# A state-space layer whose elementwise steps take one operand from PSUM, in a new order of steps

## The chip, the cores and the metric

The kernel runs on one core of a Trainium2 chip. The engines that matter are TensorE (PE, with its weight loads PEld), VectorE (DVE), ScalarE (ACT), GpSimd (POOL) and SyncE (SP), which issues DMAs. Each engine runs its own instructions in their order; between engines, semaphores make one wait for another. The metric is the time of one execution on the device, in microseconds: the median of three runs.

## The reference

The kernel computes a trunk of two layers on 512 tokens of 1024 features: a mixer, a layer norm, a SwiGLU feed-forward part and a layer norm, twice. The mixer of the second layer is attention; that of the first is the state-space layer to which the change is confined. Cut to what matters:

```python
mag = exp(lam_re * dt); lbar = mag * (cos, sin)(lam_im * dt)       # 64 groups, 64 complex states each
coef = (lbar - 1) / lam;  bb = coef * b
bu = einsum('blgh,gph->lbgp', u, bb)                                # 16 inputs a group
s  = associative_scan(s_t = lbar * s_{t-1} + bu_t)                  # along the 512 positions
y  = Re(einsum('lbgp,ghp->blgh', s, c)) + d_skip * x
h  = gelu(y); val, gate = split(h @ w_glu, 2); z = val * sigmoid(gate)
mix = z @ w_out
```

## The kernel before

Positions are cut into 64 chunks of 8. Within a chunk the output comes from a kernel K_t = Re(C lambda^t B) of 8 lags; from chunk to chunk the state is carried by a scan. Groups are handled in 4 blocks of 8 groups a half (`GB` = 8). The tiles have 128 partitions and 1024 floats, and one such step on DVE handles one tile.

For each block b, the function `ssm` (L460) has small functions that each issue one step. `f_g` (L617) and `f_h` (L626) make the tables G = powers x B and H = powers x C, two parts each (letters g, j and h, i); each part is an outer product, three DVE instructions (`outer`, L597): a product into the tile, a second product into a scratch tile `u`, their sum. `p_t` transposes G on PE (letters t, T; L636, the copy back on ACT L637). `p_m` (m, M; L647) multiplies it with the input into PSUM banks 2 and 3. `p_k` (k; L673) computes the kernel, ACT copies it to the tile `ksb` (L680), POOL adds the diagonal, and SP writes it to DRAM (`kd`, L682). `f_n` (n; L690, L696) reads it back with 8 DMAs of shifted rows (16 for block 3). `f_e` (e; POOL, L466 by a helper) makes the exponentials, `f_r` (r) rotates PSUM's v by them on DVE, and `f_s` (s) runs the scan (L742), a POOL memset of the first column (L745), and four products and sums into the state tile `s`. `p_y` (y; L766) multiplies states and kernels into y, in PSUM banks 4 and 5, ACT copies it to `ysb` (L774). `p_z` (z; L781) transposes back, ACT applies gelu (L786) and rounds to the high part `xh` (L789); `f_l` (l) makes the low part `xl` on DVE. B stands for the powers of the later blocks (DVE), b for the exponentials' tables of the later blocks (`levels`, POOL, L1144).

Between these steps the dense product of the GLU starts. It comes in 32 quarters (an output tile and two feature tiles), and a product of float32 numbers is three matmuls: high x high, low x high, high x low (L292 to L294). The weights are read as chunks of 512 KB, two quarters each; ACT makes the high part (`wh`, L228) and DVE the remainder (`wl`, L231): letter p. The letter u1 runs one item of `GLU_FIRST` in banks 6 and 7 with copies to SBUF (L818); w0 and w2 run one that stays in PSUM. The rest of the quarters, the sigmoid and the split of the result follow in `ssm_end` (L879), where remainders are on POOL; then `proj` (the output product, L311 to L313) and all that follows.

The order of all this is written by hand: `SSM_ORDER` is a string of steps, a letter and a block each, and for PE, DVE, ACT, POOL and SP the instructions are issued in exactly the order in which the string calls the functions (`tc.manual_schedule`). An SBUF slot comes from a ring of 37 and is waited for when the ring hands it out again.

Of the kernel before, what the change touches and what calls it, by code (L numbers as in the profile page):

```python
# [244 lines left out]
class Trunk:  # L245
    def __init__(self, tc, io, ctx):
# [213 lines left out]
    def ssm(self):  # L460
        """The state-space layer, its GLU and output product. State rows are (half of the groups, p);
        blocks of GB groups of either half give the feature tiles b and 4 + b."""
# [146 lines left out]
        def tab(t, b):
            return (t[0], slice(0, GB)) if b == 0 else (t[GB], slice((b - 1) * GB, b * GB))  # L610

        def f_g(b, c=0, ns=None):
            gs = slice(b * GB, b * GB + GB)
# [1 line left out]
            if len(g) <= c:
                g.append(ring.get("g", F32))
            n0 = st[b].get(("n", c), 0)  # L617
            ns = slice(n0, ns or L)
            outer(g[c], (gt_[:, 0, gs], gt_[:, 1, gs]), (bre, bim), gs, c, 1, ns)
            st[b]["n", c] = ns.stop  # L620
# [8 lines left out]
        def p_t(b, c=0):
            """Transposes of G's part c."""  # L630
            g = st[b]["g"]
            gt = st[b]["gt", c] = ring.get("gt", F32)
            for hf in range(2):
                pt = self.ps[:, hf].rearrange("p (j m) -> p j m", j=4)
                for j in range(4):
                    nc.tensor.transpose(out=pt[:, j], in_=g[c][:, (hf * 4 + j) * 128:(hf * 4 + j + 1) * 128], identity=ident)  # L636
# [598 lines left out]
```

## Time and profile before

| | |
|---|---|
| time of one execution, median of 3 | 1273.83 us (1273.69 to 1274.01) |
| profiled execution, its span | 1271.4 us |
| outside the span (median less span) | 2.4 us |
| busy: PE, DVE, ACT, POOL | 1189.0, 691.3, 421.5, 224.2 us |
| state-space stage, up to the last product of y | 178.2 us |

PE is busy for 94% of the span. The stage of the state-space layer is the first seventh of it. A row of the timeline reads: start in us, length, engine, line, operation, output <- inputs, in brackets the idle time ahead of it and what ended it. In the prediction the lines of before are numbers of the old file; the changed file's numbers are 2 to 6 larger for the same code.

### The profile page before, as it was taken

The page shows a single profiled execution, that of the slowest core. Times are in us where ns is not written, and L with a number is a line of the kernel's source. Part 1 is how long each engine was busy: PE and PEld are TensorE (multiplying, and loading weights), DVE is VectorE, ACT ScalarE, POOL GpSimd, SP SyncE. Part 2 cuts the span into 40 slices and gives each one's busy share as a digit, 9 for nine tenths or more (in the row PEclk, how much of TensorE's full clock was granted, in tenths as well). Part 3 has the DMA queues.
Part 4 walks back from the last instruction along what each step waited for, and adds up shares of the span by engine and source line. Part 5 has one row for each costly group of instructions (what it writes and reads, how often), then busy time and mean ns, then how long its engine had stood idle before and what let it go on. Part 6 is the DMA issues. An engine that isn't in the chain of part 4 may idle for free.

```text
span 1271.4 us, 16542 instructions
## 1 busy us (share of the span) xinstructions
PE 1189.0 (94%) x6804; PEld 986.4 (78%) x6804; DVE 691.3 (54%) x1030; ACT 421.5 (33%) x588; POOL 224.2 (18%) x217
## 2 busy tenths in 40 slices
PE   3269899999999999999999999999999999999996
PEld 2157678898888888888897788877988888888885
DVE  8859776772333333322777877877623333333236
ACT  1134344233232222322136666553322222223200
POOL 6982206330000000001024222223300000000000
PEclk9589999999999999999999999999999999999998
DMA  4524474132222223434022112122423222234301
GB/s 135 108 42 86 84 259 139 67 132 84 83 77 73 83 83 105 138 125 130 26 75 61 47 60 67 56 94 100 163 70 99 80 70 83 83 115 139 111 18 50
DMA packets 44332, 117.51 MB, mean 92 GB/s; under 512 B 6368, under 2 KB 17760, under 8 KB 44128
## 3 DMA queue, kind: packets, MB, share of 16 engines
q1 hardware_dynamic: 44256, 116.46, 30.0%
q8 instruction: 53, 0.87, 0.3%
q14 instruction: 23, 0.19, 0.1%
HBM read 112.38 MB, written 4.06 MB: 92 GB/s over the span
## 4 chain that ended last, share of the span: by engine, by line
PE 78%; DVE 5%; ACT 2%; POOL 0%; issue 0%; DMA 0%; DVEq 0%; POOLq 0%; ACTq 0%
PE psum L294 16%; PE psum L292 16%; PE psum L293 16%; PE psum L312 8%; PE psum L311 8%; PE psum L313 8%; DVE nb L999 1%; PE psum L1021 1%; PE psum L1086 1%; PE psum L1088 1%; PE psum L1087 1%; PE psum L1037 1%; PE psum L1036 1%; ACT wh L228 1%; DVE wl L231 1%; PE psum L985 1%
## 5 line engine op out<-in xcount | busy, mean ns | idle before, releaser
L293 PE MATMUL psum<-xh,wl 128*128 128x512 f32 (+1 forms) x1056 | 392.9, 373 | 4.8 <-DVE wl L231 4.8
L292 PE MATMUL psum<-xh,wh 128*128 128x512 f32 (+1 forms) x1056 | 395.0, 375 | 0.7 <-ACT xh L287 0.7
L294 PE MATMUL psum<-xl,wh 128*128 128x512 f32 (+1 forms) x1056 | 394.0, 374 | 0.0
L228 ACT ACTIVATE wh<-raw 128x1024 fp32r<-128x1024 f32 x188 | 194.4, 1054 | 231.1 <-PE psum L313 68.7
L231 DVE TENSOR_TENSOR wl<-raw,wh 128x1024 fp32r<-128x1024 f32 x159 | 198.7, 1279 | 126.3 <-ACT wh L228 98.3
L293 PEld LDWEIGHTS psum<-xh,wl 128*128 128x128 f32 x1056 | 198.8, 188 | 40.9 <-DVE wl L231 5.6
L292 PEld LDWEIGHTS psum<-xh,wh 128*128 128x128 f32 x1056 | 198.6, 188 | 38.4 <-issue 2.4
L294 PEld LDWEIGHTS psum<-xl,wh 128*128 128x128 f32 x1056 | 198.4, 188 | 33.5
L410 DVE TENSOR_TENSOR s<-s,psum 128x512 f32<-128x512 f32 x44 | 30.3, 688 | 278.7 <-PE psum L294 278.7
L231 POOL TENSOR_TENSOR wl<-raw,wh 128x1024 fp32r<-128x1024 f32 x29 | 73.2, 2542 | 456.3 <-DMA raw<-w_v 317.2
L313 PE MATMUL psum<-wh,hid 128*128 128x512 f32 x352 | 137.6, 391 | 0.0
L311 PE MATMUL psum<-wh,hid 128*128 128x512 f32 x352 | 137.4, 390 | 0.0
L312 PE MATMUL psum<-wl,hid 128*128 128x512 f32 x352 | 137.4, 390 | 0.0
L287 ACT ACTIVATE hid<-s 128x512 fp32r<-128x512 f32 x44 | 27.7, 629 | 172.4 <-DVE s L410 172.4
L313 PEld LDWEIGHTS psum<-wh,hid 128*128 128x128 f32 x352 | 66.1, 188 | 14.2
L311 PEld LDWEIGHTS psum<-wh,hid 128*128 128x128 f32 x352 | 66.1, 188 | 13.8
L312 PEld LDWEIGHTS psum<-wl,hid 128*128 128x128 f32 x352 | 66.1, 188 | 13.7
L1000 POOL TENSOR_TENSOR be<-be,nb 128x768 f32<-128x768 f32 (+1 forms) x24 | 49.4, 2059 | 97.9 <-DVE nb L999 82.3
L999 DVE TENSOR_TENSOR_SCAN nb<-nb,dm 128x384 f32<-128x384 f32 (+1 forms) x48 | 49.9, 1081 | 9.7 <-ACT nb L994 6.9
L409 ACT ACTIVATE s<-psum 128x512 f32<-128x512 f32 x44 | 26.2, 595 | 74.4 <-PE psum L294 74.3
L636 PE MATMUL psum<-ident,g 128*128 128x128 f32 x64 | 12.1, 350 | 40.9 <-DVE g L466 20.6
L288 DVE TENSOR_TENSOR hid<-s,hid 128x512 fp32r<-128x512 f32 x44 | 30.5, 693 | 32.2 <-ACT hid L287 32.2
(179 smaller groups left out, 1441.6 us busy)
## 6 DMA issues: line engine op xcount, KB each, us to landing
raw<-w_gu SPq DMA_DIRECT2D x88, 512.0 KB, 3.6
raw<-w_down SPq DMA_DIRECT2D x44, 512.0 KB, 3.6
raw<-w_glu SPq DMA_DIRECT2D x16, 512.0 KB, 4.6
raw<-w_qk SPq DMA_DIRECT2D x16, 512.0 KB, 3.6
raw<-w_out SPq DMA_DIRECT2D x8, 512.0 KB, 4.8
raw<-w_v SPq DMA_DIRECT2D x8, 512.0 KB, 3.6
raw<-w_o SPq DMA_DIRECT2D x8, 512.0 KB, 3.5
xres<-xs SPq DMA_DIRECT2D x4, 512.0 KB, 7.3
```

Of the source, the lines that this page charges most:

```text
L228: nc.scalar.activation(h, w, AF.Copy)
L231: (self.l_eng or nc.vector).tensor_tensor(out=l, in0=w, in1=h.bitcast(F32), op=SUB)
L288: self.nc.vector.tensor_tensor(out=l, in0=src, in1=h.bitcast(F32), op=SUB)
L292: mm(out=out, lhsT=sh, rhs=mh, start=first, stop=False)
L293: mm(out=out, lhsT=sl, rhs=mh, start=False, stop=False)
L294: mm(out=out, lhsT=sh, rhs=ml, start=False, stop=last)
L311: mm(out=o, lhsT=sh[:, ts], rhs=hl[0][:, c], start=first, stop=False)
L312: mm(out=o, lhsT=sh[:, ts], rhs=hl[1][:, c], start=False, stop=False)
L313: mm(out=o, lhsT=sl[:, ts], rhs=hl[0][:, c], start=False, stop=last)
L410: nc.vector.tensor_tensor(out=s, in0=s, in1=self.ps[:, b + 1], op=MUL)
L999: V.tensor_tensor_scan(nb[:, h], nb[:, h], dm[u], 0.0, MUL, ADD)
L1000: G_.tensor_tensor(out=be, in0=be, in1=nb, op=MUL)
```

## The change

1. The second product of an outer product goes into PSUM (banks 4 and 5, called `U`) instead of an SBUF tile, and the power tables that it multiplies are read from PSUM bank 1 (`ptab`), into which ACT copies them for each block (new letter c, `a_c`; the table for block 0 is written there by DVE itself). B and C stay in SBUF.
2. Rotation and scan: the second product goes to `U`, the sum to banks 2 and 3 (`V_`), the scan writes to `U`, the products behind it use `V_`. So each of these DVE steps reads one operand in SBUF and one in PSUM. The memset of the state tile moves from POOL to DVE.
3. y and z move from banks 4 and 5 to banks 2 and 3, the transposes' second half from bank 1 to bank 6. The diagonal is added by PE (four small matmuls with the identity) instead of by POOL.
4. Remainders of weights: letter p now makes them on POOL, a new letter q on DVE; in `ssm_end` they move from POOL to DVE.
5. The end of the GLU works in place in PSUM.
6. A new `SSM_ORDER`, and a new division of the GLU's quarters: 20 ahead of `ssm_end` instead of 18.

```diff
 GLU_FIRST, GLU_LAST = glu_items(
-    "30 50 10 40 60 51 41 11 201 312 0012 70 612")
+    "30 50 10 40 60 20 51 41 21 001 112 312 7012 612")
 SSM_ORDER = (
-    "e0 g0 j0 h0 t0 i0 T0 M0 m0 B0 k0 r0 g1 j1 b0 s0 t1 h1 i1 p e1 g2 T1 d2 n0 M1 y0 z0 e2 l0 k1 j2 m1 p "
-    "r1 s1 t2 u1 n1 u1 T2 u1 p g3 e3 m2 h2 u1 M2 y1 i2 t3 p z1 u1 k2 l1 u1 j3 n2 r2 p u1 u1 u1 s2 h3 i3 "
-    "y2 T3 z2 p l2 p k3 p M3 n3 m3 r3 s3 u1 u1 p p p y3 p w0 p p z3 l3 w2 p p"
+    "c0 e0 g0 j0 t0 h0 T0 b0 i0 m0 M0 e1 k0 n0 r0 s0 p y0 B0 c1 p g1 t1 z0 j1 T1 l0 u1 e2 p u1 h1 m1 M1 i1 k1 n1 u1 "
+    "p r1 u1 s1 y1 c2 g2 p u1 j2 z1 t2 T2 h2 u1 m2 M2 i2 l1 k2 n2 p r2 u1 u1 a e3 p s2 y2 c3 g3 u1 p j3 z2 t3 T3 h3 "
+    "u1 a m3 M3 i3 l2 k3 n3 r3 p u1 u1 p s3 y3 p w0 q a z3 w4 l3 q q"
 )
...
+        ptab = [self.ps[:, 1, i * 256:i * 256 + 256].rearrange("p (t a g n) -> p t a g n", t=2, a=2, n=L)
+                for i in range(2)]
+        U = self.ps[:, 4:6]
+        V_ = self.ps[:, 2:4]
...
+        def a_c(b):
+            t, o = tab(pwt, b)
+            if b:
+                nc.scalar.activation(ptab[b % 2][:, 0], gt_[:, :, b * GB:b * GB + GB], AF.Copy)
+            nc.scalar.activation(ptab[b % 2][:, 1], t[:, 1:3, o, 1:], AF.Copy)
...
-            u = ring.get("u", F32)
-            o, v = (v4(t)[:, :, ns] for t in (o, u))
+            o, v = v4(o), v4(flat(U))
...
             tt(o, p0, a0, MUL)
             tt(v, p1, a1, MUL)
             tt(o, o, v, SUB if (sign > 0) == (part == 0) else ADD)
-            ring.put(u)
...
+                    if not lo:
+                        nc.tensor.matmul(out=kp[:, slot, 0:16], lhsT=ident, rhs=dd[:, b, slot], start=False, stop=True)
...
-            tt(k4[:, :, 0:16], dd[:, b], k4[:, :, 0:16], ADD, G_)
...
-            tt(w2, e2(0), v2, MUL)
-            tt(x2[:, ::-1], e2(1), v2, MUL)
-            tt(w2[:, 0], w2[:, 0], x2[:, 0], ADD)
-            tt(w2[:, 1], w2[:, 1], x2[:, 1], SUB)
+            tt(w2, e2(0), V_, MUL)
+            tt(U[:, ::-1], e2(1), V_, MUL)
+            tt(V_[:, 0], w2[:, 0], U[:, 0], ADD)
+            tt(V_[:, 1], w2[:, 1], U[:, 1], SUB)
...
-            V.tensor_tensor_scan(x, r8, w, 0.0, MUL, ADD)
+            V.tensor_tensor_scan(flat(U), r8, flat(V_), 0.0, MUL, ADD)
...
-            G_.memset(s.rearrange("p (a c) -> p a c", c=NCH)[:, :, 0:1], 0.0)
+            V.memset(s.rearrange("p (a c) -> p a c", c=NCH)[:, :, 0:1], 0.0)
...
-            yp = self.ps[:, 4:6].rearrange("p a (j t) -> p (a j) t", j=4)
+            yp = V_.rearrange("p a (j t) -> p (a j) t", j=4)
...
+        def pump(e):
+            ws.l_eng = e
+            ws.pump(ws.split)
+            ws.l_eng = None
...
-            self.ws.l_eng = self.nc.gpsimd
             self.ws.pump(self.c_glu[i, qs[-1]][0] + 2 + n)
-            self.ws.l_eng = None
```

Since the order is written as a string, three places of it are shown as they reach the engines.

ACT, from the copy of block 0's kernel (`ksb`) on; `r_...` are the decay tiles, `gt` the transposed tables, `hg` the gelu. Before:

```order
L680 ACTIVATE ksb_411<-psum 128x512
L637 ACTIVATE gt_466<-psum 128x512 x2
L228 ACTIVATE wh_493<-raw_487 128x1024
L718 ACTIVATE r_43_501<-pk_93 128x16x63
L637 ACTIVATE gt_515<-psum 128x512 x2
L774 ACTIVATE ysb_600<-psum 128x4x8x16 x2
```

and now:

```order
L686 ACTIVATE ksb_433<-psum 128x512
L228 ACTIVATE wh_462<-raw_456 128x1024
L776 ACTIVATE ysb_516<-psum 128x4x8x16 x2
L610 ACTIVATE psum<-pk_96 128x128
L611 ACTIVATE psum<-pk_87 128x128
L228 ACTIVATE wh_539<-raw_458 128x1024
L641 ACTIVATE gt_549<-psum 128x512 x2
```

Block 1's transposed tables (`gt_466`, `gt_515`) were copied ahead of block 0's `ysb`; now the copies of block 1's power tables (L610, L611), and all that follows from them, stand behind it.

SP, around block 0's kernel. Before:

```order
L682 DMA kd<-ksb_411 128x4x128
L215 DMA raw_487<-w_glu 128x1024
L215 DMA raw_489<-w_glu 128x1024
L215 DMA raw_491<-w_glu 128x1024
L215 DMA raw_497<-w_glu 128x1024
L690 DMA xl<-kd 16x16x128 x8
```

and now:

```order
L687 DMA kd<-ksb_433 128x4x128
L695 DMA xl<-kd 16x16x128 x8
L215 DMA raw_456<-w_glu 128x1024
L215 DMA raw_458<-w_glu 128x1024
L215 DMA raw_460<-w_glu 128x1024
```

The first weight chunks moved behind the reads of the kernel.

POOL, from the last rows of the later blocks' tables (`levels`) on. Before:

```order
L1144 TENSOR_TENSOR scr_79<-pk_93 128x2x96 x2
L1144 TENSOR_TENSOR pk_93<-scr_79 128x48x4
L745 MEMSET s_460 128x16
L466 TENSOR_TENSOR e_499<-pk_93,pk_90 128x512
L466 TENSOR_TENSOR eu_500<-pk_93,pk_90 128x512
```

and now:

```order
L1163 TENSOR_SCALAR pk_93<-pk_93 128x24x2
L1150 TENSOR_TENSOR scr_79<-pk_93 128x2x96 x2
L1150 TENSOR_TENSOR pk_93<-scr_79 128x48x4
L466 TENSOR_TENSOR e_354<-pk_93,pk_90 128x512
L466 TENSOR_TENSOR eu_355<-pk_93,pk_90 128x512
```

The memset of block 0's state tile no longer stands behind the tables; it is on DVE, in front of the products that follow the scan.

More of the change, by code (lines that the diff above doesn't have):

```diff
@@ L587, in powers @@
             tt(gu_[:, :, gs], p[:, 0:2, :, 0:L], b8(cfi), MUL)
-            tt(gt_[:, :, gs], gt_[:, :, gs], gu_[:, :, gs], ADD)
+            tt(ptab[0][:, 0] if gs is first else gt_[:, :, gs], gt_[:, :, gs], gu_[:, :, gs], ADD)
         powers(first)
@@ L595, in ssm, with tab, outer @@
         st = [dict() for _ in range(NBLK)]
-        def outer(o, pw, a, gs, part, sign, ns=slice(0, L)):
-            n = ns.stop - ns.start
-            u = ring.get("u", F32)
-            o, v = (v4(t)[:, :, ns] for t in (o, u))
-            p0, p1 = (t[:, :, ns].unsqueeze(3).to_broadcast([128, GB, n, 16]) for t in pw)
-            a0, a1 = (t[:, gs].unsqueeze(2).to_broadcast([128, GB, n, 16]) for t in (a if part == 0 else a[::-1]))
+        def tab(t, b):
+            return (t[0], slice(0, GB)) if b == 0 else (t[GB], slice((b - 1) * GB, b * GB))
+        def a_c(b):
[3 more added lines that the diff above has]
+            nc.scalar.activation(ptab[b % 2][:, 1], t[:, 1:3, o, 1:], AF.Copy)
+        def outer(o, pw, a, gs, part, sign):
+            o, v = v4(o), v4(flat(U))
+            p0, p1 = (pw[:, i].unsqueeze(3).to_broadcast([128, GB, L, 16]) for i in range(2))
+            a0, a1 = (t[:, gs].unsqueeze(2).to_broadcast([128, GB, L, 16]) for t in (a if part == 0 else a[::-1]))
             tt(o, p0, a0, MUL)
@@ L606, in outer, with f_g @@
             tt(o, o, v, SUB if (sign > 0) == (part == 0) else ADD)
-            ring.put(u)
[L609 to L613, printed above, removed]
-            g = st[b].setdefault("g", [])
[L615 to L620, printed above, removed]
+        def f_g(b, c=0):
+            g = st[b].setdefault("g", [])
+            g.append(ring.get("g", F32))
+            outer(g[c], ptab[b % 2][:, 0], (bre, bim), slice(b * GB, b * GB + GB), c, 1)
         def f_h(b, c=0):
-            gs = slice(b * GB, b * GB + GB)
             h = st[b].setdefault("h", [])
             h.append(ring.get("h", F32))
-            t, o = tab(pwt, b)
-            outer(h[c], (t[:, 1, o, 1:], t[:, 2, o, 1:]), (cre, cim), gs, c, -1)
+            outer(h[c], ptab[b % 2][:, 1], (cre, cim), slice(b * GB, b * GB + GB), c, -1)
         def p_t(b, c=0):
@@ L675, in p_k @@
                                              rhs=hh[rows, j, 0:L - 1].rearrange("p n h -> p (n h)") if lo else c0[rows, g0 + j],
-                                             start=c == 0, stop=c == 1)
+                                             start=c == 0, stop=c == 1 and lo > 0)
+                    if not lo:
+                        nc.tensor.matmul(out=kp[:, slot, 0:16], lhsT=ident, rhs=dd[:, b, slot], start=False, stop=True)
             g_done(b)
@@ L749, in f_s @@
             tt(s4[:, 1, :, hi], s4[:, 1, :, hi], w4[:, 1, :, lo], ADD)
-            ring.put(w, x, e, r8)
+            ring.put(e, r8)
             st[b]["s"] = s
@@ L829, in glu_end @@
             s = self.tmp.tile([128, S], F32, tag="s", name="s")
+            z, y = self.ps[:, banks], self.ps[:, banks + 1]
             if i in part:
-                z = part[i][0][:, :S]
-                tt(s, part[i][0][:, S:], self.ps[:, banks + 1], ADD)
-                nc.scalar.activation(s, s, AF.Sigmoid)
-                tt(z, z, self.ps[:, banks], ADD)
-                tt(s, s, z, MUL)
-                ring.put(part[i][0])
-            else:
-                nc.scalar.activation(s, self.ps[:, banks + 1], AF.Sigmoid)
-                tt(s, s, self.ps[:, banks], MUL)
+                p = part[i][0]
+                tt(y, p[:, S:], y, ADD)
+                nc.scalar.activation(s, y, AF.Sigmoid)
+                tt(z, p[:, :S], z, ADD)
+                ring.put(p)
+            else:
+                nc.scalar.activation(s, y, AF.Sigmoid)
+            tt(z, s, z, MUL)
             zt[i] = ring.get("zt")
-            self.split(zt[i][:, 0:S], zt[i][:, S:], s)
+            self.split(zt[i][:, 0:S], zt[i][:, S:], z)
         first = list(GLU_FIRST)
@@ L864, in ssm @@
                     glu_add()
-                elif w == "p":
-                    ws.pump(ws.split)
-                elif w == "L":
-                    ws.load(ws.loaded)
+                elif w in "pq":
+                    pump(G_ if w == "p" else V)
                 else:
@@ L880, in ssm_end @@
         for n, (i, qs) in enumerate(GLU_LAST):
-            banks = (0, 2, 4, 6)[n % 4]
+            banks = (0, 4, 2, 6)[n % 4]
             self.glu(i, qs, banks, start=n > 1)
             self.glu_end(i, banks)
-            self.ws.l_eng = self.nc.gpsimd
             self.ws.pump(self.c_glu[i, qs[-1]][0] + 2 + n)
-            self.ws.l_eng = None
         self.proj(self.c_out, self.zt, nxt, order=[i for i, _ in GLU_LAST])
```

27 lines of the change are left out of this document (14 added, 13 removed).

## The prediction

> **What bounds the kernel now.** I read the page's first line, the windows table of the first 220 us, and then the timelines of the engines in the state-space stage. Everything behind that stage is untouched, so the question is when the stage hands over to the dense products.
>
> ```profile
> span 1271.4 us, 16542 instructions
> 40.00:60.00 20.00, 7.13 (x56) 6.21 (x56) 19.69 (x16) 4.26 (x6) 19.25 (x24) 0.50 0.85 171
> 60.00:80.00 20.00, 8.57 (x88) 5.33 (x88) 12.49 (x10) 0.60 (x1) 19.65 (x18) 0.61 0.00 1
> 160.00:180.00 20.00, 19.12 (x146) 13.84 (x145) 14.45 (x13) 6.96 (x10) 2.48 (x1) 1.00 0.69 187
> 180.00:200.00 20.00, 20.00 (x94) 16.48 (x93) 10.38 (x11) 14.20 (x15) 7.20 (x3) 1.00 0.80 301
> 200.00:220.00 20.00, 20.00 (x89) 16.43 (x88) 16.28 (x17) 8.58 (x12) 10.47 (x4) 1.00 0.35 124
> ```
>
> Columns: window, its length, busy PE, PEld, DVE, ACT, POOL, granted clock, DMA share, GB/s. From 180 us on PE is busy all 20.00 of 20.00 us. Between 40 and 80 us it is busy for 15.7 of 40 at a granted clock of 0.50 to 0.61, with POOL (39 of 40) and DVE the busy ones.
>
> ```profile
> 14.86 1.25 DVE L466 TENSOR_TENSOR g<-pk,bb 128x1024 f32<-128x1024 f32 x1
> 30.86 0.57 PE L673 MATMUL psum<-h,g 64*32 64x112 f32 x16
> 71.45 0.12 POOL L745 MEMSET s<- 128x16 f32 x1
> 71.63 1.12 PE L766 MATMUL psum<-h,s 64*64 64x128 f32 x8 [11.43 <-POOL s L745]
> 79.93 0.65 PE L766 MATMUL psum<-h,s 64*64 64x128 f32 x8
> 102.41 0.39 PE L766 MATMUL psum<-xh,xres 128*64 128x128 f32 x4
> 170.61 0.94 PE L766 MATMUL psum<-h,s 64*64 64x128 f32 x8 [0.81 <-DVE s L466]
> 177.57 0.65 PE L766 MATMUL psum<-h,s 64*64 64x128 f32 x8
> ```
>
> Block 0's kernel product k0 is over at 31.4, but its output product y0 starts at 71.6, because a small memset of the state tile stands behind a long list of POOL instructions. Output product y3 ends at 177.57 + 0.65 = 178.2. The same products follow it in both kernels (17 quarters of the GLU's 32, and the transposes z3), and PE has no gap there. **So the end moves one for one with the end of y3, as long as what follows keeps PE fed.** My sum is the new end of y3.
>
> **The change, part by part.** First, the contention. DVE's steps with two SBUF sources and POOL's work slow each other:
>
> ```profile
> 18.69 1.10 POOL L1144 TENSOR_TENSOR pk<-scr 128x16 f32<-128x16 f32 x1
> 30.92 0.31 POOL L1144 TENSOR_TENSOR pk<-scr 128x16 f32<-128x16 f32 x1
> 38.84 2.49 POOL L466 TENSOR_TENSOR e<-e,eu 128x512 f32<-128x512 f32 x2
> 126.79 3.50 DVE L466 TENSOR_TENSOR w<-w,x 128x512 f32<-128x512 f32 x2
> 42.61 1.63 DVE L466 TENSOR_TENSOR w<-w,x 128x512 f32<-128x512 f32 x2
> 133.49 2.28 DVE L742 TENSOR_TENSOR_SCAN x<-r,w 128x1024 f32<-128x1024 f32 x1
> 139.43 1.22 DVE L466 TENSOR_TENSOR h<-pk,cc 128x1024 f32<-128x1024 f32 x1
> 106.19 1.22 DVE L466 TENSOR_TENSOR g<-pk,bb 128x1024 f32<-128x1024 f32 x1
> 109.72 1.22 DVE L466 TENSOR_TENSOR h<-pk,cc 128x1024 f32<-128x1024 f32 x1
> ```
>
> One POOL form takes 1.10 us beside the outer products and 0.31 without them; one DVE pair 3.50 against 1.63. An outer product of three steps, undisturbed, takes 109.72 - 106.19 = 3.53 us; scan with the three or four steps behind it 139.43 - 133.49 = 5.94, and with the memset that comes to DVE (0.12 on POOL) 6.1. The rotation ahead of the scan I take as 3.65: two products at the spacing of those steps (2.25) and the pair at 1.4. [...]
>
> What a PSUM operand costs is seen for a source, not for a destination:
>
> ```profile
> L466 DVE TENSOR_TENSOR w<-e,psum 128x1024 f32<-128x1024 f32 x4 | 4.8, 1211 | 5.4 <-POOL e L466 5.4
> L466 DVE TENSOR_TENSOR g<-pk,bb 128x1024 f32<-128x1024 f32 x8 | 10.4, 1303 | 0.0
> 105.05 1.22 DVE L231 TENSOR_TENSOR wl<-raw,wh 128x1024 fp32r<-128x1024 f32 x1
> ```
>
> 1211 ns with a PSUM source, 1220 in the undisturbed rows without. For PSUM writes I take no difference either, with bounds of -1% (the 1211) and +10%: 1.35 us for 1.22, a little over the contended group's 1303. [...]
>
> **The new loop.** The power tables now come into PSUM by ACT copies, c(b+1), that stand behind the copies of y(b) in ACT's queue, and DVE's outer products of block b+1 wait for them. Before, DVE worked a block ahead while y(b) waited; now the blocks run one after the other: y(b), ysb, c(b+1), four outer products, k(b+1), the copy ksb, the write of the kernel to DRAM, eight reads of it, y(b+1). The second cycle, through the banks that V shares with y and z, is inside it. Prices:
>
> ```profile
> 150.11 0.32 PE L673 MATMUL psum<-cc,g 64*32 64x16 f32 x16
> 152.28 2.45 PE L647 MATMUL psum<-xres,gt 128*64 128x64 f32 x64
> 86.58 0.58 ACT L680 ACTIVATE ksb<-psum 128x512 f32<-128x512 f32 x1
> 88.36 0.38 SPq L682 DMA_DIRECT2D kd<-ksb  x1
> 90.83 3.75 SPq L690 DMA_DIRECT2D xh<-kd  x8
> xh<-kd SPq DMA_DIRECT2D x2, 128.0 KB, 7.4
> 140.58 0.44 PE L766 MATMUL psum<-xl,xres 128*64 128x128 f32 x4
> 148.21 1.09 PE L636 MATMUL psum<-ident,g 128*128 128x128 f32 x8
> 150.21 2.09 ACT L786 ACTIVATE hg<-psum 128x512 f32<-128x512 f32 x2 [0.22 <-PE psum L781]
> 152.33 1.06 ACT L789 ACTIVATE xh<-hg 128x1024 fp32r<-128x1024 f32 x1
> 148.33 0.60 ACT L774 ACTIVATE ysb<-psum 128x512 f32<-128x512 f32 x1 [3.22 <-PE psum L766]
> 85.78 1.24 DVE L466 TENSOR_TENSOR xl<-hg,xh 128x1024 fp32r<-128x1024 f32 x1 [13.18 <-ACT xh L789]
> 88.06 0.48 PE L292 MATMUL psum<-xh,wh 128*128 128x512 f32 x1
> 93.65 1.03 PE L636 MATMUL psum<-ident,g 128*128 128x128 f32 x8
> ```
>
> k takes 152.28 - 150.11 = 2.2; y on a warm PE 148.21 - 140.58 = 7.6 and on a cold one 79.93 + 0.65 - 71.63 = 8.9; a half copy 0.6. The two table copies of 128x128 have no row: between nothing and two such half copies, 0 to 1.2; being a quarter of its size each, 0.55 for both. The round trip through DRAM: write at 88.36, last read issued by 94.14 (90.83 + 3.75 less the last one's length) and landed 7.4 later, so 101.5; from the issue of the write 13.1. POOL's diagonal add, which is now a PE product inside k, stood ahead of it; with 0.2 of latency I take 13.3 from ksb's end. A GLU quarter is 12 matmuls: two of them 93.65 - 88.06 = 5.6, one 2.8.
>
> *Block 0.* g0 starts with the powers at 14.86 as before; four outer products end at 14.86 + 4 x 3.53 = 29.0 and k0 at 31.3 (31.4 before, so nothing gained), ksb 32.1, reads landed 45.4. POOL's exponentials, the four pairs up to 41.3 before, come ahead of the long list; with them ready by 31 the rotation and scan end at 31.2 + 3.65 + 6.1 = 41, hidden. y0 runs 45.5 to 54.1: 26 us earlier than 80.6. The raw chunks, four loads of 512 KB ahead of the reads before, now stand behind them.
>
> *Block 1.* ysb and the copies 0.7 + 0.55, c1 at 55.4; g1 and j1 to 62.6; l0 waits 1.9 for xh (gelu 2.1, copy 1.0 behind z0) and takes 1.1; h1, i1 to 72.7. On PE z0, the transposes, two quarters, m1 and M1 hold k1 to 76.4. ksb 77.2, landed 90.5, y1 to 98.3. Between k1 and y1 PE waits 8 us.
>
> *Block 2.* c2 99.5, four outer products 113.8, k2 116.1, ksb 116.9, landed 130.2, y2 to 138.0, with 8 us of PE wait again.
>
> *Block 3.* c3 139.2, i3 153.5; PE has a double quarter (5.6) ahead of m3, M3, and k3 ends at 158.4. Now two double quarters and 0.8 of waiting for their copies fill PE to 170.2, while the first eight reads of block 3 land at about 169.6. y3 from 170.2 to 177.8.
>
> Sum: 177.8 - 178.2 = **-0.4 us**. The 26 us gained in block 0 are spent at some 42 us a block, against 31, 38 and 30 before (y's first rows at 71.6, 102.4, 140.6, 170.6). Behind y3 the remainders of ssm_end, 10 of them on POOL before, are DVE's now: 10 x 1.2 (the 105.05 row) = 12 us more in a window of 47, in which it had 10.38 and 16.28 of each 20. That is near 43 of 47 at the most, which can hold a quarter up here and there; I add 1 (0 to 5). z3 with its gelu is covered by the double quarter w4 (5.6 against 2.1 + 1.0 + 1.2 + hand-overs). Errors of such a sum are mostly waits that I have missed, so I add 0.6 more: +1.2 in all. The timed median, 1273.83, is 2.4 above the profiled span; the same lies around both, so 1273.8 + 1.2 = **1275.0**.
>
> **The rivals.** *Faster: the loop turns quicker.* If the DRAM trip takes 12 us (no weight loads between, no POOL add) every block gains 1.3, and y3 ends at about 174: -4, 1269.8. With 11 and outer products at 3.4 each, near -7. For it: the raw loads moved behind the reads. Against: block 1 had one raw load between and took 13.1, block 2 much the same; and in block 3 PE's own work bounds y3 from k3 on. *Slower: writes to PSUM are dear.* The place is the loop's DVE part: 3.9 us instead of 3.53 an outer product, scan part 7.0, rotation 4.3 give y3 at 181.9, so +3.7, and 1277.5 to 1279 with the DVE window behind it. It decides as soon as a step is more than 5% longer. *The contention stays.* POOL's list for the later blocks then takes 28 us rather than the 13.5 that I give it, late exponentials hold the rotation, and y3 ends near 180.5: +2.7, 1276.5 to 1278. *Slower: the GLU's end starves.* Waits for DVE's remainders behind y3, +5 at most, decides when DVE has more than 47 us of work there.
>
> **How the numbers follow.** About 0.2% (2.5 us) is what this kernel's times can tell from no change. Forecast, within 1271.3 and 1276.4: 0.36. The quicker loop 0.29. The three on the slow side, which add up, 0.35 (PSUM writes 0.14, contention 0.08, starved end 0.13). The range reaches from the quicker loop's -8 to the slow ones together, +12: 1266 to 1286; the forecast's own range is 1271 to 1278.
>
> **What would show it.** After the change: y0's L768 row starts near 45 with a DMA as releaser; L610/L611 copies directly behind ysb, and DVE's first step of a block waiting 10 to 15 us for ACT's psum; PE waits of about 8 us ahead of y1 and y2 on DMA xh or xl; y3's last row near 178; undisturbed outer products at 1.22 a step with POOL busy beside them; no PE wait on DVE wl above 1 us behind y3. I am wrong if blocks take under 40 us or over 44 from one y to the next, or if PE has gaps after 180.

## The result, and the profile after

The changed kernel takes 1286.01 us (1285.11 to 1286.66, four runs) against 1273.76 (1273.41 to 1274.01) for the kernel before on the same chip: a ratio of 1.0098 with a 95% interval of 1.0084 to 1.0113. It is 12.3 us slower. The forecast was 1275.0, no change.

The first line of the changed kernel's page, and then its windows table (columns as in the prediction: window, length, busy PE, PEld, DVE, ACT, POOL, granted clock, DMA share, GB/s).

```profile
span 1284.9 us, 16590 instructions
```

```profile
40.00:60.00 20.00, 10.50 (x96) 6.52 (x96) 14.20 (x18) 3.68 (x6) 11.27 (x11) 0.67 0.71 186
60.00:80.00 20.00, 15.94 (x164) 13.32 (x164) 14.32 (x14) 10.64 (x14) 10.32 (x9) 0.76 0.00 1
...
180.00:200.00 20.00, 19.73 (x149) 14.51 (x149) 3.09 (x2) 5.22 (x7) 8.84 (x4) 1.00 0.82 284
```

Between 40 and 80 us PE is busy for 26.4 of 40 us, against 15.7 before, and POOL for 21.6 against 39: the hole of the kernel before is smaller. From 180 us on PE has work nearly throughout (19.73 of 20.00), as before. The loss is between these two. The rows of PE at the output products y, and of ACT and DVE behind them, say where:

```profile
46.15 0.69 PE L768 MATMUL psum<-xl,xres 128*64 128x128 f32 x4 [13.32 <-DMA xl<-kd]
55.99 0.65 PE L768 MATMUL psum<-h,s 64*64 64x128 f32 x8
96.96 0.70 PE L768 MATMUL psum<-xh,xres 128*64 128x128 f32 x4 [8.57 <-DMA xh<-kd]
105.48 0.65 PE L768 MATMUL psum<-h,s 64*64 64x128 f32 x8
106.98 0.28 ACT L611 ACTIVATE psum<-pk 128x128 f32<-128x128 f32 x1
107.30 1.23 DVE L466 TENSOR_TENSOR g<-psum,bb 128x1024 f32<-128x1024 f32 x1 [18.83 <-ACT psum L611]
140.72 0.69 PE L768 MATMUL psum<-xl,xres 128*64 128x128 f32 x4 [9.27 <-DMA xl<-kd]
149.49 0.65 PE L768 MATMUL psum<-h,s 64*64 64x128 f32 x8
183.81 0.44 PE L768 MATMUL psum<-tn,xres 128*64 128x128 f32 x4
191.19 0.65 PE L768 MATMUL psum<-h,s 64*64 64x128 f32 x8
```

In the kernel before, y0 did not begin at 71.6, the row that the prediction shows. Its first four products stand 12 us earlier, and the rest waited for the memset:

```profile
59.51 0.69 PE L766 MATMUL psum<-xl,xres 128*64 128x128 f32 x4 [2.49 <-DMA xl<-kd]
```

So starts can't be compared between the two kernels (the 31 us that the prediction gives for the first round before are 42.9 from this row on), but ends can. y0 now ends at 55.99 + 0.65 = 56.6 instead of 80.6, 24 us earlier. From one y's end to the next it takes 49.5, 44.0 and 41.7 us (before: 33.2, 34.5, 30.0), and y3 ends at 191.19 + 0.65 = 191.8 instead of 178.2. These 13.6 us are the whole loss (the spans differ by 13.5). From start to start the changed kernel's blocks follow each other at 50.8, 43.8 and 43.1 us. The first product of the output projection begins 47.9 us behind y3, before it was 47.6.

The prices of the steps stand in these groups of the stage (line, engine, operation and tile, count | busy us, mean ns of one | idle time before and what ended it); the last row is POOL's in the kernel before:

```profile
L466 DVE TENSOR_TENSOR psum<-psum,bb 128x1024 f32<-128x1024 f32 x8 | 9.8, 1223 | 0.0
L466 DVE TENSOR_TENSOR psum<-e,psum 128x1024 f32<-128x1024 f32 x4 | 4.9, 1222 | 0.0
L1150 POOL TENSOR_TENSOR scr<-pk 128x16 f32<-128x16 f32 (+5 forms) x24 | 8.2, 365 | 0.3
L682 PE MATMUL psum<-pk,ident 128*128 128x16 f32 x32 | 6.5, 277 | 0.0
L1144 POOL TENSOR_TENSOR scr<-pk 128x16 f32<-128x16 f32 (+5 forms) x24 | 22.8, 971 | 0.3
```

The DVE steps that write PSUM take 1.22 us here, what the undisturbed ones that write SBUF took (1.22). POOL's table steps fell from 971 ns (22.8 us for 24) to 365. So the DVE steps with a PSUM operand got no dearer and POOL's tables lost their contention; the time went elsewhere. Some contention stayed, off the path: the powers of the later blocks (B0, operands in SBUF) now run on DVE beside POOL's tables and exponentials and take 13.1 us (39.12 to 52.25) where they took 5.4, but DVE then still waits 5.6 us for the table copies of block 1.

### The profile page after: what moved, and what is told of

The parts are those of the page before. It is cut to its first block, busy times and chain, and to the rows that moved or that the text cites. A ratio compares the mean times of both kernels' runs of the same rounds, so it can differ in the third digit from the quotient of the medians.

```text
span 1284.9 us, 16590 instructions
## 1 busy us (share of the span) xinstructions
PE 1200.5 (93%) x6832; PEld 995.6 (77%) x6832; DVE 670.1 (52%) x1032; ACT 423.4 (33%) x597; POOL 192.9 (15%) x212
## 4 chain that ended last, share of the span: by engine, by line
PE 84%; DVE 9%; DMA 3%; ACT 2%; issue 1%; SPq 1%; POOL 0%; DVEq 0%; POOLq 0%; ACTq 0%
PE psum L294 16%; PE psum L292 16%; PE psum L293 16%; PE psum L312 8%; PE psum L313 8%; PE psum L311 8%; PE psum L768 3%; DVE nb L1005 1%; DVE g L466 1%; DMA xl<-kd 1%; PE psum L1027 1%; DVE psum L466 1%; PE psum L1092 1%; PE psum L677 1%; SPq L695 1%
## 5 line engine op out<-in xcount | busy, mean ns | idle before, releaser
L231 DVE TENSOR_TENSOR wl<-raw,wh 128x1024 fp32r<-128x1024 f32 x157 | 195.6, 1274 | 131.6 <-ACT wh L228 103.5
L231 POOL TENSOR_TENSOR wl<-raw,wh 128x1024 fp32r<-128x1024 f32 x31 | 76.3, 2477 | 557.3 <-DMA raw<-w_v 317.2
L287 ACT ACTIVATE xh<-psum 128x512 fp32r<-128x512 f32 x24 | 14.0, 596 | 96.8 <-PE psum L357 93.3
```

The lines of the kernel that those rows point to most:

```text
L231: (self.l_eng or nc.vector).tensor_tensor(out=l, in0=w, in1=h.bitcast(F32), op=SUB)
L287: self.nc.scalar.activation(h, src, AF.Copy)
```

## The experiments

The sum of the prediction put y3's end at 177.8; it came 14.0 later. Laying its steps beside the trace gives this list:

| step | by the sum | measured | difference over the blocks |
|---|---|---|---|
| kernel product k (blocks 1 to 3; block 0's end) | 2.2 each; 31.3 | 4.0 each; 32.8 | 1.5 + 3 x 1.8 = 6.9 |
| y0, y1, y2, y3 | 8.6, 7.8, 7.8, 7.6 | 10.5, 9.2, 9.4, 8.0 | 5.3 |
| block 1, from y0's end to k1 | 20.1 | 22.0 | 1.9 |
| k's end to y's start, four times | 14.2, 14.1, 14.1, 11.8 | 13.3, 14.3, 15.0, 11.1 | -0.5 |
| the other blocks, from y's end to k | 15.6, 18.2 | 15.6, 18.5 | 0.3 |

From it comes the **theory**: the loop is the predicted one, two of its prices were too low (k, with its four pairs of identity products, and the products behind a wait, which run at a lower clock: the granted clock was 0.50 from 97.00 to 100.30 us, at the start of y1), and what eats block 0's gain of 24 us is the order, in which a block waits for the block before it. **Rivals**: PE's later waits would absorb these microseconds whatever they cost; the order is not the cause but the ACT copies of the tables, which a kernel with tables in SBUF would not need; or the useful part of the change is the moved memset alone, and the rest is loss.

| kernel | median us (lowest to highest) | ratio to before, 95% | end of y3 |
|---|---|---|---|
| before, beside the changed kernel (1273.21 to 1273.55 beside the others) | 1273.76 (1273.41 to 1274.01) | | 178.2 |
| changed | 1286.01 (1285.11 to 1286.66) | 1.0084 to 1.0113 | 191.8 |
| diag_dve | 1280.77 (1280.05 to 1281.05) | 1.0041 to 1.0071 | 186.2 |
| warm | 1287.87 (1285.57 to 1291.74) | 1.0095 to 1.0137 | 192.0 |
| diag_warm | 1281.59 (1280.64 to 1283.17) | 1.0050 to 1.0080 | 188.3 |
| warm2 | 1283.70 (1281.90 to 1286.79) | 1.0072 to 1.0106 | 187.4 |
| diag_warm2 | 1277.68 (1277.28 to 1279.07) | 1.0024 to 1.0053 | 182.6 |
| memset | 1278.82 (1277.02 to 1279.06) | 1.0027 to 1.0052 | 183.9 |
| memset_diag | 1270.83 (1269.97 to 1273.29) | 0.9972 to 0.9991 | 175.6 |
| look | 1268.59 (1266.64 to 1268.81) | 0.9944 to 0.9974 | 173.6 |
| look_diag | 1266.29 (1265.88 to 1267.26) | 0.9931 to 0.9960 | 171.1 |
| ord8 | 1254.48 (1253.16 to 1256.13) | 0.9838 to 0.9867 | 156.0 |
| ord8_sbuf | 1287.55 (1286.27 to 1291.09) | 1.0101 to 1.0131 | 185.9 |
| after_sbuf | 1296.12 (1295.02 to 1297.67) | 1.0160 to 1.0194 | 200.1 |

In look, look_diag, ord8 and ord8_sbuf the same code stands two or three lines higher in the file, so that the helper's L466 is L464 there.

### The diagonal taken off PE

```diff
-                                             start=c == 0, stop=c == 1 and lo > 0)
-                    if not lo:
-                        nc.tensor.matmul(out=kp[:, slot, 0:16], lhsT=ident, rhs=dd[:, b, slot], start=False, stop=True)
+                                             start=c == 0, stop=c == 1)
...
-            nc.scalar.activation(k4, kp, AF.Copy)
+            nc.scalar.activation(k4[:, :, 16:], kp[:, :, 16:], AF.Copy)
+            tt(k4[:, :, 0:16], dd[:, b], kp[:, :, 0:16], ADD)
```

In the changed kernel the identity products are left out, and one DVE step adds the diagonal to the first 16 columns as it reads them from PSUM.

> The changed kernel, but the diagonal is added by one small DVE step that reads PSUM (128x64), not by PE's small products inside k. Theory (mis-sized k): in the changed kernel k takes 4.0 us where 2.2 was assumed, and 1.8 us a block stand on the loop; without them k is 2.2 to 2.4 long, y3 ends 6 to 7 us earlier than 191.8, and the time is about 1279.5 us. Rival (k is long because PE's clock has fallen, the diagonal products cost next to nothing): k stays above 3.3 us and the time is 1284 us or more.

5.2 us less (6.5 expected). The timeline of PE shows the price: first two of the four rounds of k2 in the changed kernel, then two of k1 without the identity products.

```profile
122.70 0.29 PE L677 MATMUL psum<-cc,g 64*32 64x16 f32 x16
122.93 0.39 PE L682 MATMUL psum<-pk,ident 128*128 128x16 f32 x2
123.25 0.59 PE L677 MATMUL psum<-h,g 64*32 64x112 f32 x16
123.66 0.29 PE L677 MATMUL psum<-cc,g 64*32 64x16 f32 x16
```

```profile
78.48 0.29 PE L677 MATMUL psum<-cc,g 64*32 64x16 f32 x16
78.60 0.57 PE L677 MATMUL psum<-h,g 64*32 64x112 f32 x16
78.99 0.29 PE L677 MATMUL psum<-cc,g 64*32 64x16 f32 x16
```

A round takes 123.66 - 122.70 = 0.96 us with the pair and 78.99 - 78.48 = 0.51 without; four rounds make the 1.8 us that k was too long. y3 comes 5.6 us earlier: the rival that a later wait absorbs it is out.

### Keeping PE's clock up

Dummy products (the identity by itself, letter d) are put ahead of y0, y1 and y2. The first form meant 70, 55 and 60 of them, but a step's number is one digit, so 7, 5 and 6 were issued; the second strings together what was meant to fill the wait.

```diff
-... p y0 ... s1 y1 ... s2 y2 ...
+... p d70 y0 ... s1 d55 y1 ... s2 d60 y2 ...
```

> The changed kernel with 70, 55 and 60 products that nothing reads ahead of y0, y1 and y2, where PE waits for the kernel's reads. Theory (cold clock): after each wait y runs at half clock for 3 to 4 us, 9.2 to 10.5 us instead of 7.65, so three y's and block 1's transposes get 1.5 to 2 us shorter each; y3 ends about 5 to 6 us earlier, the time is about 1280.5 us. Rival (the clock is not what makes y long): y stays above 9 us, the time is 1286 us or, where the dummies end late, up to 1289 us.

> Both edits together. If k's products and the cold clock are the two terms that the prediction missed, they add up, -12 us: y3 ends near 180 and the time is 1274 us, what the prediction's sum gave (1275). If a third term is missing, 1278 us or more stays.

Seven products fill about 1 us of a wait of 13. The waits stayed (6.67 us ahead of y1), y1 took 9.4 us as before, and neither time differs from that of its kernel without dummies beyond the scatter. These two say nothing on the theory.

```diff
-... p y0 ... s1 y1 ... s2 y2 ...
+... p d9 d9 d9 d9 d9 y0 ... s1 d9 d9 d9 d2 y1 ... s2 d9 d9 d9 d4 y2 ...
```

> The changed kernel with 45, 29 and 31 products that nothing reads ahead of y0, y1 and y2; the earlier run with this aim issued 7, 5 and 6 only, since a step's number is one digit, and left waits of 6.7 to 12.6 us. One of them took 0.26 us, so these fill 12, 7.5 and 8 us. Theory (cold clock): y0 to y2 take 7.7 to 8.2 us instead of 9.2 to 10.5, block 1's transposes 1.0 instead of 1.9, y3 ends 4 to 6 us earlier, time 1280 to 1282 us. Rival (the clock does not set y's length): y stays above 9 and the time within 1 us of 1286.

The windows around y1 and y2, in the changed kernel and then in warm2, and rows of warm2's PE at y0 and y1:

```profile
87.90:106.20 18.30, 9.73 (x100) 5.95 (x99) 0.56 (x1) 1.22 (x3) 1.77 (x1) 0.81 0.69 103
130.00:150.20 20.20, 10.93 (x104) 6.83 (x103) 2.50 (x4) 3.68 (x6) 13.51 (x10) 0.75 0.81 155
```

```profile
87.90:106.20 18.30, 16.72 (x166) 13.39 (x165) 1.47 (x2) 3.41 (x7) 1.65 (x2) 1.00 0.64 101
130.00:150.20 20.20, 17.90 (x174) 14.20 (x172) 3.54 (x4) 5.43 (x10) 11.56 (x10) 1.00 0.66 140
```

```profile
46.50 0.70 PE L768 MATMUL psum<-xl,xres 128*64 128x128 f32 x4 [3.75 <-DVE scr L1150]
96.21 0.44 PE L768 MATMUL psum<-xh,xres 128*64 128x128 f32 x4 [1.58 <-DMA xh<-kd]
103.25 0.65 PE L768 MATMUL psum<-h,s 64*64 64x128 f32 x8
```

The granted clock around y1 and y2 rises from 0.81 and 0.75 to 1.00, and y1 takes 103.25 + 0.65 - 96.21 = 7.7 us instead of 9.2; y2 likewise 7.7 instead of 9.4. Ahead of y0 the dummies ended 3.75 us too early, and y0 was slow again (10.1; the granted clock was 0.76 from 43 to 57 us). y3 ends 4.4 us earlier. The time fell by 2.3 us, less than the expected 4 to 6, with intervals that overlap the changed kernel's, so the trace shows this effect and the time alone does not. With the diagonal on DVE as well, and 55, 31 and 41 dummies:

> The changed kernel with the diagonal on DVE and 55, 31 and 41 products that nothing reads ahead of y0, y1 and y2 (0.23 us each in the run before, so 12.6, 7.1 and 9.4 us). If the diagonal products and the cold clock are the two terms that the prediction's sum lacked, both come off: y3 ends near 180.5 against the sum's 177.8 and the kernel's 191.8, and the time is 1274 to 1277 us against the predicted 1275.0. If a third term is missing, it stays above 1279 us.

1277.68 us, and y0, y1 and y2 take 7.7 us each: 8.3 of the 11.0 us by which the forecast was missed are back. The time is 0.7 us above the expected 1274 to 1277, and y3 ends at 182.6, 2.1 later than expected and still 4.8 behind the sum. About 3 of that lie between y0 and k1 (76.70 - 53.45 = 23.3 us against 20.1), where PE waits for DVE and then works at the lower clock:

```profile
60.00:80.00 20.00, 17.44 (x240) 14.06 (x240) 10.68 (x11) 11.12 (x15) 7.46 (x7) 0.78 0.01 2
58.70 1.94 PE L640 MATMUL psum<-ident,g 128*128 128x128 f32 x8 [5.24 <-DVE g L466]
105.98 1.09 PE L640 MATMUL psum<-ident,g 128*128 128x128 f32 x8 [1.00 <-DVE g L466]
```

The same eight transposes take 1.94 us behind a wait of 5.24 and 1.09 behind one of 1.00. Another 1.6 are in block 2's trip through DRAM (k2's end 119.26 to y2 134.94, 15.7 against 14.1).

### The kernel before with single parts of the change

In the kernel before, the memset of the state tile goes from POOL to DVE; in the second kernel the diagonal also goes from POOL to DVE, read from PSUM as in diag_dve.

```diff
-            G_.memset(s.rearrange("p (a c) -> p a c", c=NCH)[:, :, 0:1], 0.0)
+            V.memset(s.rearrange("p (a c) -> p a c", c=NCH)[:, :, 0:1], 0.0)
```

> The kernel before with one thing of the change alone: the memset of the state tile on DVE instead of POOL. Theory: block 0's gain can be had without the new order; y0 no longer waits for POOL's list and starts near 60 us (its reads' landing), DVE's 13 us wait for xh goes, later blocks move up by 8 to 11 us and the time is about 1265 us. Rival (the stage is bound elsewhere, as by DVE's contended steps): 1272 to 1274 us.

> The kernel before with the memset on DVE and the diagonal added by DVE from PSUM; order and SBUF tables as before. With the memset alone y0 came 13 us earlier but block 1's diagonal waited 24.7 us on POOL behind exponentials. Theory (POOL's queue is what held block 1): the kernel of block 1 is written near 74 instead of 95, y1 starts by 100 and the time is 1264 to 1270 us. Rival (DVE and POOL, contending, hold block 1 anyway): r1 and s1 end as late as with the memset alone, y1 starts at 103 to 108, and the time is 1274 to 1279 us.

The memset alone moves y0's end from 80.6 to 67.7 and still makes the kernel 5.5 us **slower** than the kernel before in the same batch (1273.34); neither the theory's 1265 us nor the rival's 1272 to 1274 came. The timelines of memset's POOL, DVE and SP show the reason:

```profile
73.74 2.08 POOL L466 TENSOR_TENSOR eu<-pk,pk 128x512 f32<-128x512 f32 x1
74.78 2.12 DVE L466 TENSOR_TENSOR g<-pk,bb 128x1024 f32<-128x1024 f32 x1
93.99 1.24 POOL L466 TENSOR_TENSOR ksb<-pk,ksb 128x64 f32<-128x64 f32 x1
95.25 0.38 SPq L682 DMA_DIRECT2D kd<-ksb  x1
```

DVE, no longer held by y0, now works while POOL makes its exponentials; steps of 1.22 and 1.09 us take 2.12 and 2.08. POOL's list ends later, the add of block 1's diagonal stands behind it at 93.99 (87.24 before), and the kernel goes to DRAM at 95.25 instead of 88.36. With the diagonal off POOL too, y3 ends 2.6 us earlier than before, and the ratio is 0.9982 (0.9972 to 0.9991); the diagonal's step on DVE, the last one ahead of the write of block 1's kernel, is over when the PE row that it releases begins, at 74.44, as expected, but the time is 0.8 us above the expected 1264 to 1270. So the two small moves gain 0.2% together, and one of them alone loses 0.4%: the rival of the memset is out.

### The order

Only the order string changes: the tables, outer products and kernel product of block b + 1 come ahead of y(b) where the slots allow it. look keeps all else of the changed kernel; look_diag has the diagonal on DVE.

```diff
-    "c0 e0 g0 j0 t0 h0 T0 b0 i0 m0 M0 e1 k0 n0 r0 s0 p y0 B0 c1 p g1 t1 z0 j1 T1 l0 u1 e2 p u1 h1 m1 M1 i1 k1 n1 u1 "
-    "p r1 u1 s1 y1 c2 g2 p u1 j2 z1 t2 T2 h2 u1 m2 M2 i2 l1 k2 n2 p r2 u1 u1 a e3 p s2 y2 c3 g3 u1 p j3 z2 t3 T3 h3 "
-    "u1 a m3 M3 i3 l2 k3 n3 r3 p u1 u1 p s3 y3 p w0 q a z3 w4 l3 q q"
+    "c0 e0 g0 j0 t0 h0 T0 b0 i0 m0 M0 B0 e1 k0 n0 r0 s0 p c1 g1 j1 y0 t1 h1 T1 z0 i1 p k1 n1 l0 m1 M1 e2 p c2 u1 u1 "
+    "r1 s1 p u1 g2 u1 t2 j2 T2 u1 y1 h2 p i2 u1 z1 k2 n2 l1 m2 M2 e3 p c3 u1 u1 r2 s2 u1 g3 t3 j3 a p T3 u1 y2 h3 p "
+    "i3 z2 k3 n3 l2 m3 M3 a p u1 r3 s3 u1 p y3 p w0 q a z3 w4 l3 q q"
```

> The changed kernel with a new order string only: the power tables, the outer products and the kernel of block b+1 are issued ahead of y(b) on every engine (c(b+1) ahead of ysb(b) on ACT), and block 0's powers ahead of its scan on DVE. Theory (the serial loop through c(b+1), the outer products and the DRAM trip is what eats block 0's gain): blocks then follow at DVE's own pace, about 25 to 30 us instead of 42 to 50, y3 ends between 145 and 160 instead of 191.8, and the time is 1240 to 1256 us. Rival (the stage is bound by PE's work and clock, or by the weight stream): y3 stays beyond 175 and the time above 1270 us.

> The same order, and the diagonal added by a DVE step from PSUM instead of PE's small products. If the DRAM trip still bounds some block, k's 1.8 us a block come off it: 3 to 6 us less than the new order alone. If DVE bounds it, the new steps, which wait for k on DVE, make it 0 to 3 us slower than that.

look gains 17.4 us on the changed kernel, and that by order alone; it is also faster than the kernel before (ratio 0.9944 to 0.9974). The gain is smaller than expected (1240 to 1256 us, and y3's end by 160 instead of 173.6). What is left shows in its timeline:

```profile
47.91 1.06 ACT L226 ACTIVATE wh<-raw 128x1024 fp32r<-128x1024 f32 x1 [14.65 <-DMA raw<-w_glu]
48.88 0.26 ACT L608 ACTIVATE psum<-pk 128x128 f32<-128x128 f32 x1
102.51 0.65 PE L766 MATMUL psum<-h,s 64*64 64x128 f32 x8
106.92 0.32 PE L675 MATMUL psum<-cc,g 64*32 64x16 f32 x16
```

Block 1's table copies stand on ACT behind the rounding of a weight chunk that waits 14.65 us for its DMA, and k2 stands on PE behind y1 (end 103.2), a GLU quarter and z1. With the diagonal on DVE the median is 2.3 us lower, with intervals that overlap (y3 ends 2.5 earlier). In look_diag the diagonal's DVE steps wait for the copy of k: 29.1 us in three waits, because DVE now comes to them early.

ord8 is look_diag with an order searched further, in which tables of up to two blocks ahead come into PSUM early and k1 and k2 have fewer products of the GLU ahead of them:

```diff
+    "c0 g0 e0 b0 e1 t0 m0 p j0 h0 i0 T0 M0 e2 B0 k0 c1 r0 g1 s0 c2 j1 h1 n0 t1 y0 T1 i1 g2 z0 k1 m1 p t2 j2 l0 n1 M1 "
+    "r1 c3 u1 u1 s1 h2 g3 i2 u1 T2 p y1 t3 z1 u1 k2 p p e3 j3 l1 u1 m2 M2 p u1 u1 r2 n2 u1 s2 h3 y2 T3 z2 a p i3 u1 "
+    "k3 l2 m3 M3 u1 n3 r3 u1 p s3 y3 a p p u1 p w0 q a z3 w4 l3 q q"
```

> The kernel of the earlier order with the diagonal on DVE, and an order string that goes further: outer products and transposes up to two blocks ahead, k2 and its DRAM write as early as its operands allow, the table copies on ACT ahead of anything that waits for a weight chunk. In the earlier order DVE still waited 6.3, 3.5, 14.8 and 10.8 us (for ACT's copies behind a late chunk, and for k2 and k3, which stood on PE behind y1 and y2). Theory (what is left of the stage is order, not work): those waits mostly go, y3 ends 8 to 16 us earlier than 171.1, the time is 1250 to 1258 us. Rival (PE's own work and the DRAM trips bound the stage by now): 1263 us or more.

1254.48 us: 31.5 below the changed kernel, and 18.7 below the kernel before in the same batch (1273.21, ratio 0.9838 to 0.9867). It beats both, and it lies within the expected 1250 to 1258. Two of its waits of PE up to y3 (engine, line <- what ended it: us, times, longest):

```profile
PE psum L638 <- DVE g L464: 29.9, 2, 19.3
PE psum L765 <- DMA xl<-kd: 5.1, 1, 5.1
```

Of the three waits for the kernel's trip through DRAM (13.3, 8.6 and 9.3 us in the changed kernel) one of 5.1 is left. Behind y3 PE has no gap (46.00 us busy of the 46 up to 202). The 19.3 are the wait for the first tables (16.8 in the kernel before, 19.1 in the changed one).

### Tables and second products back in SBUF

In ord8 and in the changed kernel's own order, `outer` reads its tables from SBUF and puts the second product into an SBUF tile again; the ACT copies fall away, and the rest stays (rotation and scan in PSUM, too).

```diff
-            o, v = v4(o), v4(flat(U))
-            p0, p1 = (pw[:, i].unsqueeze(3).to_broadcast([128, GB, L, 16]) for i in range(2))
+            u = ring.get("u", F32)
+            o, v = v4(o), v4(u)
+            p0, p1 = (pw[i].unsqueeze(3).to_broadcast([128, GB, L, 16]) for i in range(2))
...
+            ring.put(u)
```

> The same order with the tables and the second products of the outer products back in SBUF, as in the kernel before, so that DVE's outer products read SBUF twice again (rotation, scan and sums stay in PSUM). It tells the worth of the PSUM operands from that of the order. Theory (contention costs): POOL's tables and exponentials take 1.5 to 2 times as long beside the outer products, and single DVE steps 1.3 to 2 us beside POOL; with DVE close to the bound here the time is 4 to 12 us above that of the same order with PSUM operands. Rival (the order alone does it): within 2 us of it.

> The changed kernel in its own order with tables and second products of the outer products back in SBUF (rotation, scan and sums stay in PSUM). ACT's table copies go too, so DVE no longer waits for them. Two effects against each other. Theory: in block 0, POOL's exponentials, slowed by the outer products, are ready at 41 instead of 29, so y0 starts 6 to 8 us later than 46.2; in block 1 nothing is won, as the step for xl stands ahead of the outer products for H; in blocks 2 and 3 the outer products run while y1 and y2 wait, DVE's 18.8 us waits for ACT's copies go, and k2 and k3 come 4 to 6 us earlier each. Sum -1 to -6 us: 1280 to 1285 us, and y to y about 44 us for block 1 but under 41 for blocks 2 and 3. Rival (contention is all there is to it): y0 late by 7 and nothing won back, 1291 to 1296 us. Rival (neither matters in this order): 1286 us.

ord8 loses 33.1 us by it (4 to 12 were expected), the changed kernel 10.1. The groups of the second products in ord8, then in ord8_sbuf, with those of POOL's table steps:

```profile
L464 DVE TENSOR_TENSOR psum<-psum,bb 128x1024 f32<-128x1024 f32 x8 | 9.8, 1223 | 0.0
L1147 POOL TENSOR_TENSOR scr<-pk 128x16 f32<-128x16 f32 (+5 forms) x24 | 8.3, 368 | 0.3
```

```profile
L464 DVE TENSOR_TENSOR u<-pk,bb 128x1024 f32<-128x1024 f32 x8 | 16.6, 2070 | 8.0 <-POOL e L464 8.0
L464 DVE TENSOR_TENSOR h<-pk,cc 128x1024 f32<-128x1024 f32 x8 | 12.7, 1584 | 13.8 <-PE psum L765 13.8
L1147 POOL TENSOR_TENSOR scr<-pk 128x16 f32<-128x16 f32 (+5 forms) x24 | 16.4, 707 | 0.3
```

The contention is back: 2.07 us for 1.22, 707 ns for 368. The 33 us are not its price alone, though: `u` takes a slot of the ring, and I read the waits of 8.0 and 13.8 us for POOL and for PE's y as waits of new tiles for a slot, which no run shows. How much is slots and how much is contention was not separated.

after_sbuf decides on the ACT copies. Its forecast missed: 1296.12 us instead of 1280 to 1285, at the upper end of the rival in which contention is all (1291 to 1296). It has no copies, so DVE may go ahead of y(b). The blocks 2 and 3 still follow at 42.9 and 43.5 us from y to y (43.8 and 43.1 in the changed kernel; under 41 expected), for PE takes the steps in their order:

```profile
114.70 0.65 PE L768 MATMUL psum<-h,s 64*64 64x128 f32 x8
130.41 0.32 PE L677 MATMUL psum<-cc,g 64*32 64x16 f32 x16
```

From y1's end at 115.4 PE has z1, block 2's transposes, its m products and GLU quarters ahead of k2 at 130.4. The copies are thus not the only thing that holds a block behind the one before; the order string does so on PE as well. Of the 10 us, 9.2 were lost by the end of y1 (115.4 against 106.1). Up to there DVE's outer steps for block 1's G ran beside POOL at 2.0 to 2.3 us, and steps of the later blocks' powers took up to 2.69 us for the 0.54 of the changed kernel.

## Why the prediction was wrong

**What held.** "The end moves one for one with the end of y3": 13.6 and 13.5. y0 starts at 46.15 with the DMA as releaser (45.5 forecast). The copies c stand behind ysb, and DVE waits for them, though for 5.6 us in block 1 and 18.8 in block 2, where 10 to 15 were forecast. The gain of block 0 is eaten by the loop; at 43.8 and 43.1 us two of its rounds lie within the 40 to 44 that the prediction set as its mark, and the first, at 50.8, lies outside. Its own sum had 45.0, 39.7 and 40.0, so the mark did not fit the sum, and each round took 3 to 6 us more than the sum gave it. PE waits 8.6 and 9.3 us ahead of y1 and y2 (8 forecast). The DRAM trips are right to 0.5 us in the sum, which is partly luck: one by one they are off by -0.9, 0.2, 0.9 and -0.7. The bounds on a PSUM write were -1% to +10%, taken as nothing: 1.222 to 1.223 us for 1.22. That POOL goes undisturbed beside DVE steps with one operand in PSUM (exponentials ready by 31, 13.5 us for the list of the later blocks) was the author's assumption, and none of the prediction's rows shows it; in the changed kernel POOL's table steps take 365 ns instead of 971, the exponentials end at 26.81 + 2.51 = 29.3, and the DVE steps beside them keep to 1.22 us. Of the rivals, dear PSUM writes, staying contention and a starved end (0.3 us of 5) did not come, nor did the quicker loop. The measured 1286.01 stands at the upper end of the stated range, 1286, but that end was added up from the three slow rivals, so that it comes so near is luck.

**What failed** is two terms of the sum, together 12.2 of the 14.0 us. The first is the step "k takes 152.28 - 150.11 = 2.2", read from a k without the diagonal, while the sentence on the round trip had moved the diagonal's add "inside k" and charged it nothing: the only added PE instructions in the loop were left without a price. They cost 0.45 us a pair, 1.8 us a block, 6.9 in the table; taking them away gave 5.6 us of y3 and 5.2 us of time. The second is "y on a warm PE 148.21 - 140.58 = 7.6", which was used for y1 and y2 although the same text had them wait 8 us just before; they took 9.2 and 9.4, and y0, counted as cold at 8.6, took 10.5. The cold row it went by was too short: the 8.9 us were read from 71.63 on and leave out the four products at 59.51, and 8.6 is less again without a reason. The rows of y0 in the changed kernel show how PE runs behind the wait: from one feature tile to the next the first step is 47.82 - 46.15 = 1.67 us, later ones 53.72 - 52.77 = 0.95.

```profile
47.82 0.69 PE L768 MATMUL psum<-xl,xres 128*64 128x128 f32 x4
...
52.77 0.44 PE L768 MATMUL psum<-xl,xres 128*64 128x128 f32 x4
...
53.72 0.44 PE L768 MATMUL psum<-xl,xres 128*64 128x128 f32 x4
```

The granted clock was 0.50 from 46.15 to 50.00 us, 0.53 from 50.00 to 52.80 and 1.00 from 52.80 to 56.70. y1's slow rows last 3.4 us (from 96.96 to 100.31; the granted clock was 0.50 from 97.00 to 100.30 and 1.00 from 103.00 to 106.20), y0's 6.6 us (from 46.15 to 52.77); why y0's last twice as long was not shown. Against the 7.7 us of a y at a granted clock of 1.00 (y1 and y2 of warm2) the y behind such a wait took 1.5, 1.7 and 2.8 us more in the changed kernel (y1, y2, y0).

Block 1's 1.9 us are DVE's longer wait for `xh`, 3.72 us where the sum had 1.9:

```profile
68.67 1.22 DVE L466 TENSOR_TENSOR xl<-hg,xh 128x1024 fp32r<-128x1024 f32 x1 [3.72 <-ACT xh L791]
```

Ahead of it PE's transposes of t1 and z0 ran at the low clock (1.94 and 1.92 us at a granted clock of 0.50 from 61.57 to 65.20, against 1.09 for eight transposes in diag_warm2 behind a wait of 1.00), which makes up to 1.7 of it by estimate. But no run takes this away: in diag_warm2 DVE still waits 3.70. An ACT table load of 1.28 us ahead of the gelu (L788 at 64.16; 61.29 in diag_warm2), which the sum does not name, could hold `xh` next. This part stays open.

Both repairs together bring 1277.68, within 2.7 us of the forecast. About 3 us of what is left of the stage lie in block 1 at a clock of 0.78; that no further small wait is in it was not tested.

**"The new loop"** was the right mechanism with an incomplete cause: it was put on the ACT copies. The order change shows that the loop can be broken (17.4 us by order alone, 31.5 with a further search and the diagonal), and after_sbuf shows that it stays closed without the copies, by PE's order. For the change as it is this makes no difference; for what to do about it, it does.

## What to carry to other kernels

Give every small instruction that changes its engine a price on the new engine's own path, from the row nearest to it, and where the sum itself puts a wait ahead of a matmul group, use the cold row for that group. When a change removes a wait at the head of a chain, look next at what each engine's fixed order puts between one round and the next: here 24 us won in the first block were lost again until the steps of the next block were issued ahead of the wait. In these runs, giving DVE's steps one PSUM operand went with faster table steps on POOL (365 ns for 971) at no price to DVE (1.22 us), and taking it back cost 10.1 us in the changed kernel's order and 33.1 in ord8's (ring slots included); yet with the changed kernel's order the whole is slower than the kernel before, and with ord8's it is faster.

## What the hardware showed

- In warm2 the products behind a PE wait of 3.75 us were slow (y0, 10.1 us; the granted clock was 0.76 from 43 to 57 us); those behind waits of 1.58 and 1.92 us were not (y1 and y2, 7.7 us; the granted clock was 1.00 in both windows). The length of the wait alone does not decide it. In the kernel before, y1 waits 1.89 us, goes on at a granted clock of 1.00 (104.69 to 106.00) and then has slow rows: from 106.8 to 109.4 the granted clock is 0.50.

```profile
104.69 0.94 PE L766 MATMUL psum<-h,s 64*64 64x128 f32 x8 [1.89 <-DVE s L466]
106.82 0.69 PE L766 MATMUL psum<-xh,xres 128*64 128x128 f32 x4
```

- A pair of fp32 identity products of 128x16, put between the small tiled products of k, lengthened the round from 0.51 us (diag_dve) to 0.96 (changed kernel), more than its 0.39 us row.
- In after_sbuf and memset DVE and POOL ran steps with two SBUF sources side by side, and steps of both took longer: 2.0 to 2.3 us for 1.22 on DVE (after_sbuf, 64.55 to 77.09), and 2.08 for 1.09 on POOL (memset). In the changed kernel the steps with a PSUM source keep to 1.22 us in all groups above, and POOL's table steps beside them to 365 ns.
- An earlier start can cost time: the moved memset let DVE work beside POOL, block 1's diagonal stood behind POOL's longer list, and the kernel lost 5.5 us. With the diagonal off POOL (memset_diag) both engines were still busy nearly throughout from 60 to 80 us, DVE 19.78 and POOL 19.59 of 20, and the kernel gained 0.2%.
